# Two transformer blocks: the first four modulation weight blocks as TensorE products with silu(c) as one column

## The chip, the cores and the metric

One core of a Trainium2 chip runs the whole program; the other cores are idle. The metric is the device time of one execution in microseconds (us). Three runs of the kernel before took 1876.26, 1877.37 and 1877.62 us; the median is 1877.37 us.

## What is computed

Two blocks follow each other on a sequence of 256 positions with 1024 features. The first block is modulated by a vector `c` of 1024 numbers. What matters here is its start, layer 0:

```python
def first_block(x, c, ...):
    c_act = jax.nn.silu(c)
    h = layer_norm(x)
    for l in range(DEPTH):                              # DEPTH = 2
        ada = (c_act @ w_ada[l] + b_ada[l])[:, None, :]
        sh1, sc1, g1, sh2, sc2, g2 = jnp.split(ada, 6, axis=-1)
        u = h * (1.0 + sc1) + sh1
        y = mixer(u, w_in[l], ...)                      # z = u @ w_in, and so on
        ...
```

All arrays are float32. `w_ada[l]` is 1024 x 6144, `w_in[l]` is 1024 x 10768: the weights are by far the most data (385 MB are read in all), and the products with them most of the work.

## The kernel before, in words

**Weights.** Every weight matrix is cut on the host into chunks of 128 x 2048 numbers (1 MB), in the one order in which the kernel uses them: the list `plan` (`make_plan`, L133). SyncE loads chunk after chunk into a tile `raw` with three buffers (`emit_load`, L434; the DMA is L444 for the first three chunks, in two halves each, and L446 for all others). So a chunk can start to load when the chunk three places ahead of it has been used up. For a chunk of an ordinary matrix, ScalarE writes a rounded copy `hi` (L475, fp32r) and VectorE the remainder `lo = raw - hi` (L475); each product is then three TensorE passes: `hi` with the rounded activation `uh`, `lo` with `uh`, `hi` with the remainder `ul` (`mv_part`, L555 to L557).

**Modulation.** A chunk `("ada", l, sec, q)` holds the columns of `w_ada` for 256 of the 1024 outputs of one of the six sections, with outputs on the partitions. `ada_step` (L406) has VectorE multiply it by `crow`, silu(c) spread over all partitions, and sum over the free axis, 1024 products for 128 outputs in one instruction (L414, two to a chunk).

**The start.** `plan` begins: ada sc1 and sh1 of quarter q=0 (chunks 0 and 1), two chunks of the mixer's first products m_o and m_v (2 and 3), ada of q=1 (4 and 5), a mixer chunk (6), ada of q=2 (7, 8), two mixer chunks, ada of q=3, and so on. `norm_u0` (L836) normalizes `x` on VectorE (`bn_stats` L789, then L860), spreads `c` over the partitions with two TensorE products of a row of halves (`cbc`, L855), takes its tanh on ScalarE (L856) and builds `crow` (L862); TensorE transposes the normalized x into four PSUM banks (`tr`, L864). `step(g)` then makes the columns 2g and 2g+1 of `u`: `us` = 1 + sc (L871), one half of `uf` on VectorE (L873), the other on ScalarE (L874), the rounded `uh` on ScalarE (L877), the remainder `ul` on VectorE (L878). Each step needs one quarter of the modulation. With step 0 done, the first 24 products `mvh` can start (chunks 2 and 3, first halves); with step 1 the next ones.

**Unread products.** `busy` (L882) issues products of a tile of ones whose result nobody reads: 12 ahead of the first `mvh`, 24 behind these 24.

**Order.** The part that `norm_u0` issues is pinned: each of TensorE, VectorE and ScalarE keeps the order in which the code issues it. Behind it a scheduler of the framework places instructions by priority, and may slip some in, such as the first four products `smz` (L939) of the small gate projection. Each engine works through its own queue strictly in order.

Of the kernel before, what the change touches and what calls it, by code (L numbers as in the profile page):

```python
# [12 lines left out]
AF = mybir.ActivationFunctionType  # L13
ALU = mybir.AluOpType
AX = mybir.AxisListType

P = 128
T = 256
D = 1024
# [110 lines left out]
    return out + list(main[last:])  # L130


def make_plan():  # L133
    first = [("ada", 0, SEC[n], q) for q in range(4) for n in ("sc1", "sh1")]
    plan = []
    for l in range(DEPTH):
        m1 = spread(mixer1_chunks(l), ada_chunks(l, ["g1", "sc2", "sh2"]), *ADA1)
        plan += m1 if l else (first[:2] + m1[:2] + first[2:4] + m1[2:3] + first[4:6] + m1[3:5] +
                                 first[6:] + m1[5:])
        nxt = ada_chunks(l + 1, ["sc1", "sh1"]) if l + 1 < DEPTH else []  # L140
        plan += spread(ffn1_chunks(l), ada_chunks(l, ["g2"]) + nxt, *ADA2)
    for l in range(DEPTH):
        plan += mixer2_chunks(l) + ffn2_chunks(l)
    return plan
# [18 lines left out]
def host_arrays(inp):  # L163
# [20 lines left out]
    for i, d in enumerate(plan):  # L184
        kind, l = d[0], d[1]
        a = d[2:]
        if kind == "ada":
            c = a[0] * D + a[1] * 256 + r(256)
            o = w["w_ada"][l][:, c].T.reshape(2, P, D).transpose(1, 0, 2).reshape(P, -1)
        elif kind == "m_o":  # L190
            o = pack(w["w_in"][l], a[1] * 4 + r(4), 3072 + a[0] * 512 + r(512))
        elif kind == "m_v":
            o = pack(w["w_in"][l], a[1] * 4 + r(4), 2048 + a[0] * 512 + r(512))
        elif kind == "m_q":
            o = pack2(w["w_in"][l], k8, a[0] * 256 + r(256))
        elif kind == "m_k":
            o = pack2(w["w_in"][l], k8, 1024 + a[0] * 256 + r(256))
        elif kind == "a_v":
            o = pack(w["w_in"][l], a[1] * 4 + r(4), 4112 + 3072 + a[0] * 512 + r(512))
        elif kind == "a_qk":  # L200
            q0 = 4112 + a[1] * 512 + a[0] * 128 + r(128)
            o = pack2(w["w_in"][l], k8, np.concatenate([q0, q0 + 1536]))
        elif kind == "gab":
            o = pack(w["w_in"][l], a[1] * 4 + r(4), 4112 + 4608 + (a[0] % 2) * 1024 + (a[0] // 2) * 512 + r(512))
        elif kind == "w_b":
            o = pack(w["w_b"][l], r(4), a[0] * 512 + r(512))
        elif kind == "w_a":
            o = pack(w["w_a"][l], a[1] * 4 + r(4), a[0] * 512 + r(512))
        elif kind == "w_o":
            o = pack(w["w_out"][l], a[1] * 4 + r(4), a[0] * 512 + r(512))  # L210
        elif kind == "w13":
            c = a[0] * 128 + r(128)
            o = np.concatenate([pack(w["w1"][l], k8, c), pack(w["w3"][l], k8, c)], axis=1)
        elif kind == "w13p":
            f = np.concatenate([w[nm][l][:, P * j:P * j + P] for j in range(2) for nm in ("w1", "w3")], axis=1)
            o = pack(f, a[0] * 4 + r(4), r(512))
        elif kind == "upp":
            c = np.concatenate([o_ + P * j + r(P) for j in range(2) for o_ in (0, DFF)])
            o = pack(w["w_up_2"][l], a[0] * 4 + r(4), c)
        elif kind == "zp":  # L220
            o = pack(w["w_in_2"][l], a[0] * 4 + r(4), r(512))
        elif kind == "w2":
            o = units(w["w2"][l], w2_units(a[0]))
        elif kind == "x":
            o = pack2(w["w_in_2"][l], k8, 1024 + a[0] * 256 + r(256))
        elif kind == "k2":
            o = pack2(w["w_in_2"][l], k8, 2592 + 1024 + r(256))
        elif kind == "v2":
            o = pack(w["w_in_2"][l], k8, 2592 + 1280 + r(256))
        elif kind == "q2":  # L230
            c = np.concatenate([2592 + 64 * h + r(64) for h in order[4 * a[0]:4 * a[0] + 4]])
            o = pack2(w["w_in_2"][l], k8, c)
        elif kind == "z":
            o = pack2(w["w_in_2"][l], k8, a[0] * 256 + r(256))
        elif kind == "w_o2":
            o = units(w["w_out_2"][l][rows_o2], wo2_units(a[0]))
        elif kind == "up":
            c = a[0] * 128 + r(128)
            o = pack2(w["w_up_2"][l], k8, np.concatenate([c, DFF + c]))
        elif kind == "down":  # L240
            o = units(w["w_down_2"][l], w2_units(a[0]))
        else:
            raise ValueError(kind)
        ws[i] = o
# [59 lines left out]
def two_blocks_kernel(ctx: ExitStack, tc: tile.TileContext, a: dict, out: bass.AP, stop=None):  # L304
# [28 lines left out]
    def lbank(name):  # L333
        return lin.tile([P, 512], F32, tag="lin", name=name)
# [4 lines left out]
        nc.sync.dma_start(x[:, tt], a["x"][:, tt])  # L339
    crow = tmp([D], "crow")  # L340
    trow = tmp([D], "trow")
    c1 = tmp([D], "crow1", parts=1)
    S.dma_start(c1, a["crow"])
    S.dma_start(cst[:, :P], a["cst"][:, :P])
# [62 lines left out]
    def ada_step(d, raw):  # L407
        _, l, sec, q = d
        if q == 0:
            ada[l, sec] = tmp([8], f"adap{sec}", bufs=1)  # L410
        for i in range(2):
            ct = 2 * q + i
            src = raw[:, i * D:(i + 1) * D]
            V.tensor_tensor_reduce(src, src, crow, 1.0, pv1[l][:, 136 + sec * 8 + ct:137 + sec * 8 + ct], ALU.mult,  # L414
                                   ALU.add, ada[l, sec][:, ct:ct + 1])
        if sec not in (2, 5) or q < 3:
            return
        gt = tmp([D], "grow", bufs=2)
        col = ada[l, sec]
        ada[l, sec] = gt  # L420

        def spread_rows():
            for hf in range(2):
                ps = bank("adag")
                for c in range(4):
                    PE.transpose(ps[:, c * P:(c + 1) * P], col[:, 4 * hf + c:4 * hf + c + 1].to_broadcast([P, P]), ident)
                S.activation(gt[:, hf * 512:(hf + 1) * 512], ps, AF.Copy)

        ada_wait.append([4, spread_rows])

    ada_wait = []

    def emit_load(i, hold=None):
        d = plan[i]  # L434
# [401 lines left out]
    def norm_u0():  # L836
# [1 line left out]
        u = new_u()  # L838
        stats = tmp([2, 2, 6], "lnst")
        trs = [bank("tr") for _ in range(4)]  # L840
        sil = []
        mvs = []
        for tt in range(2):
            for hf in range(2):
# [4 lines left out]
            V.tensor_scalar(rs, mv[:, 1:2], LN_EPS, None, ALU.add)  # L849
            powm(rs, rs, 1)  # L850
            mvs.append((mv, rs))
        for hf in range(2):
            h = slice(hf * 512, (hf + 1) * 512)
            ps = lbank("cbc")
            PE.matmul(ps, halves_, c1[:, h], start=True, stop=True)  # L855
            S.activation(trow[:, h], ps, AF.Tanh)  # L856
            sil.append((h, ps))
        for tt in range(2):
            mv, rs = mvs[tt]
            V.tensor_scalar(x[:, tt, :], x[:, tt, :], mv[:, 0:1], rs, ALU.subtract, ALU.mult)  # L860
            h, ps = sil[tt]
            V.scalar_tensor_tensor(crow[:, h], trow[:, h], 1.0, ps, ALU.add, ALU.mult)  # L862
            for ct in range(8):
                PE.transpose(trs[ct // 2][:, (ct % 2) * T + tt * P:(ct % 2) * T + (tt + 1) * P],  # L864
                             x[:, tt, ct * P:(ct + 1) * P], ident)
# [11 lines left out]
            S.activation(u[0][:, c, :], uf, AF.Copy)  # L877
            V.tensor_tensor(u[1][:, c, :], uf, u[0][:, c, :].bitcast(F32), ALU.subtract)  # L878

        outs = [[lbank("mvh") for _ in range(2)] for _ in range(2)]  # L880

        def busy(o, n):  # L882

            for _ in range(n):
                PE.matmul(o[:, :P], ones, ones, start=True, stop=True)

        busy(outs[0][0], 12)
        st["cap"] = 4
        ensure(2)
        hold = []  # L890
        emit_load(2, hold)
        st["emitted"] = 3
# [1 line left out]
        step(0, hold[1])  # L894
        hold[2]()
        hold[3]()
        ws = [chunk(*d, 0) for d in EARLY[:2]]
        for w, o in zip(ws, outs):
            for tt in range(2):
                mv_part(0, w[0], tt, u, o, False, 0, 3)  # L900
        busy(trs[0], 24)
        st["cap"] = len(plan)
        return u, (step, ws, outs)

    def log1p_exp_neg(xin, n, tag):

# [65 lines left out]
    def mixer1(l, u, ob0=None, small=None, begun=None):  # L972
# [172 lines left out]
        for hp in range(2):  # L1145
# [4 lines left out]
            if l == 0:  # L1150
                if hp == 0:
                    vs = [tmp([2, 512], "mv") for _ in range(2)]
                    step, ws, obs = begun
                    dst = [oth[:, :, :512], vs[0], oth[:, :, 512:], vs[1], vt[:, 0]]
                    ensure(6)
                    step(1)
                    for i, d in enumerate(EARLY):
                        if i in (2, 4):
# [278 lines left out]
    for l in range(DEPTH):  # L1437
        pv = pv1[l]
        if l == 0:
            with pinned():  # L1440
                u, begun = norm_u0()
            stats, tail = mixer1(l, u, begun=begun)
        else:
            small = small_weights(a["wg"][l])
            u, outs = cross(tail, ln_norm(stats, u_coef(l, 0, gb)), [("m_o", l, 0, kh) for kh in range(2)],
                            TR1[0])
            for n, fn in zip((3, 6, 9, 12), affine(l - 1, 1)):
                defer(n, fn)
            stats, tail = mixer1(l, u, outs, small)
# [535 lines left out]
```

## Time and profile before

| what | value |
|---|---|
| median of three runs | 1877.37 us |
| the profiled execution, its own time | 1877.16 us |
| its span, first to last instruction | 1875.4 us |
| TensorE busy | 1847.4 us (99%) |
| VectorE busy | 1470.6 us (78%) |
| ScalarE busy | 1083.4 us (58%) |
| mean granted TensorE clock | 0.999 |
| HBM read | 384.82 MB |

The span is 1.8 us shorter than the execution's time; what lies around it is launch and end. PE is TensorE's products, PEld its weight loads, which overlap products. A TensorE instruction is recorded from its start to the end of its pipeline, so what it costs in a stream is the distance between starts, not its recorded length.

### The profile page before, as it was taken

The numbers are of one execution on the slowest core, as the hardware profiler recorded it, in microseconds if no ns is written. First come the engines' busy times: TensorE is split into PE (matmuls) and PEld (weight loads), VectorE is DVE, ScalarE is ACT, GpSimd is POOL, SyncE is SP. The second block draws the span as 40 slices with busy tenths as digits, with TensorE's granted clock in tenths as the row PEclk, the third lists the DMA queues.
The fourth block names the chain that finished last, engine by engine and source line by source line (L and its number), as shares of the span: only waits on it lengthen the run. The fifth ranks groups of instructions, "written<-read, shape, count | busy, mean of one in ns | idle before, by whom it ended". The sixth has DMA issues, their size and how long they took to land.

```text
span 1875.4 us, 31504 instructions
## 1 busy us (share of the span) xinstructions
PE 1847.4 (99%) x12422; PEld 1668.0 (89%) x12422; DVE 1470.6 (78%) x2581; ACT 1083.4 (58%) x1889; POOL 58.1 (3%) x96
## 2 busy tenths in 40 slices
PE   8999999999999999999999999999999999999998
PEld 6889988899988899988899879877999899889996
DVE  8888877788757878877876579997876599978763
ACT  4566654454445566554544456895654569956552
POOL 0000000000000000000000000000000000000000
PEclk9999999999999999999999999999999999999999
DMA  8744677467855445766477635544645465445452
GB/s 323 261 180 157 249 265 282 181 258 284 286 196 202 177 163 192 280 252 262 159 257 270 238 145 190 174 125 157 225 181 188 152 213 178 133 186 202 181 187 82
DMA packets 64341, 388.01 MB, mean 207 GB/s; under 512 B 7627, under 2 KB 12539, under 8 KB 21698
## 3 DMA queue, kind: packets, MB, share of 16 engines
q1 hardware_dynamic: 58064, 364.93, 53.2%
q0 software_dynamic: 4832, 20.13, 3.6%
q8 instruction: 97, 1.59, 0.3%
q10 hardware_dynamic: 1298, 0.95, 0.2%
q14 instruction: 50, 0.41, 0.1%
HBM read 384.82 MB, written 5.36 MB: 208 GB/s over the span
## 4 chain that ended last, share of the span: by engine, by line
PE 84%; DVE 6%; ACT 5%; issue 3%; DMA 1%; POOL 0%; POOLq 0%; DVEq 0%; ACTq 0%
PE lst L522 14%; PE lst L524 14%; PE lst L523 14%; PE ffo L616 4%; PE ffo L614 4%; PE ffo L615 4%; PE wo L615 1%; PE wo L614 1%; PE wo L616 1%; DVE lo L475 1%; PE gabl L555 1%; PE gabl L556 1%; PE gabl L557 1%; PE sy L1628 1%; PE avl L556 1%
## 5 line engine op out<-in xcount | busy, mean ns | idle before, releaser
L475 ACT ACTIVATE hi<-raw 128x1024 fp32r<-128x1024 f32 x546 | 571.7, 1057 | 486.8 <-PE lst L523 254.4
L475 DVE TENSOR_TENSOR lo<-raw,hi 128x1024 fp32r<-128x1024 f32 x546 | 662.6, 1222 | 226.2 <-ACT hi L475 222.3
L522 PE MATMUL lst<-uh,hi 128*128 128x256 f32 x2336 | 668.7, 286 | 0.4 <-DVE q2t L1786 0.4
L524 PE MATMUL lst<-uh,lo 128*128 128x256 f32 x2336 | 664.4, 284 | 0.1
L523 PE MATMUL lst<-ul,hi 128*128 128x256 f32 x2336 | 663.7, 284 | 0.0
L522 PEld LDWEIGHTS lst<-uh,hi 128*128 128x128 f32 x2336 | 447.8, 192 | 3.6 <-issue 2.1
L524 PEld LDWEIGHTS lst<-uh,lo 128*128 128x128 f32 x2336 | 447.8, 192 | 2.0 <-issue 1.2
L523 PEld LDWEIGHTS lst<-ul,hi 128*128 128x128 f32 x2336 | 448.0, 192 | 1.1 <-issue 0.3
L614 PE MATMUL ffo<-hi,ffh 128*128 128x512 f32 x352 | 137.3, 390 | 0.0
L615 PE MATMUL ffo<-lo,ffh 128*128 128x512 f32 x352 | 137.0, 389 | 0.0
L616 PE MATMUL ffo<-hi,ffl 128*128 128x512 f32 x352 | 137.0, 389 | 0.0
L414 DVE CUSTOM_DVE_ANT_0 raw<-raw,crow,pv 128x1024 f32<-128x1024 f32 x96 | 121.1, 1281 | 14.3 <-DMA raw<-in_ws_dram 14.0
L965 DVE SCALAR_TENSOR_TENSOR cacc<-cin,pv,cacc 128x254 f32<-128x254 f32 (+2 forms) x272 | 112.5, 477 | 0.2 <-ACT cacc L958 0.2
L616 PEld LDWEIGHTS ffo<-hi,ffl 128*128 128x128 f32 x352 | 66.1, 188 | 13.8
L615 PEld LDWEIGHTS ffo<-lo,ffh 128*128 128x128 f32 x352 | 66.1, 188 | 13.5
L614 PEld LDWEIGHTS ffo<-hi,ffh 128*128 128x128 f32 x352 | 66.1, 188 | 13.5
L555 PE MATMUL gabl<-hi,uh 128*128 128x512 f32 x128 | 51.2, 400 | 0.0
L557 PE MATMUL gabl<-hi,ul 128*128 128x512 f32 x128 | 50.4, 394 | 0.0
L556 PE MATMUL gabl<-lo,uh 128*128 128x512 f32 x128 | 50.3, 393 | 0.0
L1610 ACT ACTIVATE sM<-arow,ac 128x128 f32<-128x128 f32 x128 | 45.3, 392 | 0.0
L1457 ACT ACTIVATE rsq<-xres 128x512 f32<-128x512 f32 x20 | 12.5, 627 | 47.7 <-DVE xres L1932 21.6
L773 ACT ACTIVATE uf<-tr,ub,us 128x128 f32<-128x128 f32 x36 | 14.4, 452 | 36.9 <-PE tr L759 36.9
(396 smaller groups left out, 3005.9 us busy)
## 6 DMA issues: line engine op xcount, KB each, us to landing
raw<-in_ws_dram SPq DMA_DIRECT2D x329, 1024.0 KB, 4.9
abias<-in_bt_dram SPq DMA_DIRECT2D x32, 256.0 KB, 5.0
arow<-scra POOLq DMA_DIRECT2D x32, 256.0 KB, 4.6
wtab<-skew SPq DMA_DIRECT2D x16, 384.0 KB, 3.2
gb<-in_rows_dram POOLq DMA_DIRECT2D x8, 512.0 KB, 6.3
skew<-scrt POOLq DMA_DIRECT2D x4, 1024.0 KB, 11.6
raw<-in_ws_dram SPq DMA_DIRECT2D x6, 512.0 KB, 9.2
grow<-scrg POOLq DMA_DIRECT2D x2, 1024.0 KB, 6.5
```

What stands on the lines that cost most here:

```text
L414: V.tensor_tensor_reduce(src, src, crow, 1.0, pv1[l][:, 136 + sec * 8 + ct:137 + sec * 8 + ct], ALU.mult, ALU.add, ada[l, sec][:, ct:ct + 1])
L475: fn()
L522: PE.matmul(outp, sh, mh, start=first, stop=False)
L523: PE.matmul(outp, sh, ml, start=False, stop=False)
L524: PE.matmul(outp, sl, mh, start=False, stop=last)
L555: PE.matmul(outs[tt], sl[0], hi[:, i, :], start=kt == first, stop=False)
L556: PE.matmul(outs[tt], sl[0], lo[:, i, :], start=False, stop=False)
L557: PE.matmul(outs[tt], sl[1], hi[:, i, :], start=False, stop=kt == last)
L614: PE.matmul(o, sh, hi[:, i, :], start=kt in first, stop=False)
L615: PE.matmul(o, sh, lo[:, i, :], start=False, stop=False)
L616: PE.matmul(o, sl, hi[:, i, :], start=False, stop=kt in last)
L965: V.scalar_tensor_tensor(acc[:, c, lo:hi], src[:, lo + s:hi + s], cw[:, k0 + j:k0 + j + 1], acc[:, c, lo:hi], ALU.mult, ALU.add)
```

## The change

The four chunks of q = 0 and q = 1 (table `ADA_PE`) are packed as ordinary weights, with the 1024 inputs on the partitions. TensorE multiplies them with silu(c) laid out as a tile `ccol` of 128 x 8: eight products of one column for each 128 outputs, 16 to a chunk, into spare corners of PSUM banks; VectorE adds the bias of two columns in one instruction (L424 of the changed kernel). `ccol` comes from eight small products of `c` itself (`cc`), a tanh and one VectorE instruction. `crow` is still built, later, for the quarters 2 and 3 and the other sections, which stay on VectorE. The unread products are 6 ahead of the first `mvh` and 8 behind the new products of q = 1. The gate projection's weights are prepared behind the first mixer chunks, and not early as before.

```diff
+ADA_PE = [("ada", 0, SEC[n], q) for q in range(2) for n in ("sc1", "sh1")]
...
-        if kind == "ada":
+        if kind == "ada" and d in ADA_PE:
+            o = pack(w["w_ada"][l], k8, a[0] * D + a[1] * 256 + r(256))
+        elif kind == "ada":
...
+    ccol = tmp([8], "ccol")
...
+        if d in ADA_PE:
+            c = slice(2 * q, 2 * q + 2)
+            ps = ada_ps[q][:, 2 * (sec == SEC["sc1"]):][:, :2]
+            for j in range(2):
+                for k in range(8):
+                    PE.matmul(ps[:, j:j + 1], raw[:, k * 256 + j * P:k * 256 + (j + 1) * P], ccol[:, k:k + 1],
+                              start=k == 0, stop=k == 7)
+            V.tensor_tensor(ada[l, sec][:, c], ps, pv1[l][:, 136 + sec * 8 + 2 * q:138 + sec * 8 + 2 * q], ALU.add)
+            return
...
+        outs = [[lbank("mvh") for _ in range(2)] for _ in range(2)]
+        cc = outs[0][0][:, :8]
+        cbc = outs[0][1], outs[1][0]
+        ada_ps[0], ada_ps[1] = outs[1][1][:, :4], trs[0][:, :4]
+        for k in range(8):
+            PE.matmul(cc[:, k:k + 1], c1[:, k * P:(k + 1) * P], halves_[:, 0:1], start=True, stop=True)
+        for hf in range(2):
+            PE.matmul(cbc[hf], halves_, c1[:, hf * 512:(hf + 1) * 512], start=True, stop=True)
+        S.activation(ccol, cc, AF.Tanh)
+        V.scalar_tensor_tensor(ccol, ccol, 1.0, cc, ALU.add, ALU.mult)
+        for hf in range(2):
+            h = slice(hf * 512, (hf + 1) * 512)
+            S.activation(trow[:, h], cbc[hf], AF.Tanh)
+            S.activation(crow[:, h], cbc[hf], AF.Copy)
+        st["cap"] = 4
         mvs = []
...
-        for hf in range(2):
-            h = slice(hf * 512, (hf + 1) * 512)
-            ps = lbank("cbc")
-            PE.matmul(ps, halves_, c1[:, h], start=True, stop=True)
-            S.activation(trow[:, h], ps, AF.Tanh)
-            sil.append((h, ps))
         for tt in range(2):
             mv, rs = mvs[tt]
             V.tensor_scalar(x[:, tt, :], x[:, tt, :], mv[:, 0:1], rs, ALU.subtract, ALU.mult)
-            h, ps = sil[tt]
-            V.scalar_tensor_tensor(crow[:, h], trow[:, h], 1.0, ps, ALU.add, ALU.mult)
+        for tt in range(2):
+            ensure(tt + 1)
             for ct in range(8):
...
-                PE.matmul(o[:, :P], ones, ones, start=True, stop=True)
-
-        busy(outs[0][0], 12)
-        st["cap"] = 4
-        ensure(2)
+                PE.matmul(o, ones, ones, start=True, stop=True)
+
+        busy(outs[0][0][:, :P], 6)
...
         hold[3]()
+        for hf in range(2):
+            h = slice(hf * 512, (hf + 1) * 512)
+            V.scalar_tensor_tensor(crow[:, h], trow[:, h], 1.0, crow[:, h], ALU.add, ALU.mult)
+        small = small_weights(a["wg"][0])
         ws = [chunk(*d, 0) for d in EARLY[:2]]
...
-        busy(trs[0], 24)
         st["cap"] = len(plan)
-        return u, (step, ws, outs)
+        return u, (step, ws, outs, partial(busy, trs[0][:, T:T + P], 8)), small
...
                     ensure(6)
+                    busy()
                     step(1)
```

How this moves instructions shows at three places. Line numbers of the changed kernel are its own. The first is TensorE from its first product to the first `mvh`; `crow_84` and `crow_85` are the row of `c`, `raw` a weight chunk. Before:

```order
L855 MATMUL cbc<-crow_84,halves 128x512 x2
L864 MATMUL tr<-cst,xres 128x128 x16
L885 MATMUL mvh<-ones 128x128 x12
L555 MATMUL mvh<-hi,uh 128x512
L556 MATMUL mvh<-lo,uh 128x512
```

and now:

```order
L862 MATMUL mvh<-halves,crow_85 128x1 x8
L864 MATMUL mvh<-crow_85,halves 128x512 x2
L422 MATMUL mvh<-ccol,raw 128x1 x16
L888 MATMUL tr<-cst,xres 128x128 x8
L422 MATMUL mvh<-ccol,raw 128x1 x16
L888 MATMUL tr<-cst,xres 128x128 x8
L907 MATMUL mvh<-ones 128x128 x6
L571 MATMUL mvh<-hi,uh 128x512
```

Eight small products stand ahead of `cbc`, and the 32 products of chunks 0 and 1 around the first eight transposes.

The second is TensorE between the first 24 `mvh` and the next ones. Before:

```order
L557 MATMUL mvh<-hi,ul 128x512
L885 MATMUL tr<-ones 128x128 x24
L939 MATMUL smz<-uh,sw 64x256
L939 MATMUL smz<-ul,sw 32x256 x2
L939 MATMUL smz<-uh,sw 64x256
L555 MATMUL mvh<-hi,uh 128x512
```

and now:

```order
L573 MATMUL mvh<-hi,ul 128x512
L422 MATMUL tr<-ccol,raw 128x1 x32
L907 MATMUL tr<-ones 128x128 x8
L571 MATMUL mvh<-hi,uh 128x512
L572 MATMUL mvh<-lo,uh 128x512
```

The 32 products of chunks 4 and 5 come first, then eight unread ones; the four `smz` stand some 50 products further on.

The third is VectorE from step 0 to the remainders of chunk 3 (`adap` is the modulation, `sw` the gate weights). Before:

```order
L871 TENSOR_SCALAR us_191<-adap_174 128x2
L977 TENSOR_SCALAR gnh<-pv_0_99 128x8
L873 TENSOR_SCALAR uf<-tr,us_191,adap_180 128x256
L876 TENSOR_TENSOR lo<-raw,hi 128x1024
L878 TENSOR_TENSOR ul<-uf,uh 128x512
L896 TENSOR_TENSOR lo<-raw,hi 128x1024
L475 TENSOR_TENSOR lo<-raw,hi 128x1024 x2
```

and now:

```order
L424 TENSOR_TENSOR adap_155<-mvh,pv_0_100 128x2
L424 TENSOR_TENSOR adap_184<-mvh,pv_0_100 128x2
L895 TENSOR_SCALAR us_224<-adap_155 128x2
L1000 TENSOR_SCALAR gnh<-pv_0_100 128x8
L897 TENSOR_SCALAR uf<-tr,us_224,adap_184 128x256
L900 TENSOR_TENSOR lo<-raw,hi 128x1024
L902 TENSOR_TENSOR ul<-uf,uh 128x512
L916 TENSOR_TENSOR lo<-raw,hi 128x1024
L919 SCALAR_TENSOR_TENSOR crow<-trow,crow 128x512 x2
L952 TENSOR_TENSOR sw<-swr,sw 128x8x32
L491 TENSOR_TENSOR lo<-raw,hi 128x1024 x2
```

Two instructions for `crow` and one for `sw` now stand between the remainder of chunk 2 and the two of chunk 3. SyncE's and GpSimd's queues keep their order, and all engines keep theirs behind their first few hundred instructions.

## Rows read from the trace of the kernel before

**Rows 1.** The page: busy time of each engine over the span.

```profile
PE 1847.4 (99%) x12422; PEld 1668.0 (89%) x12422; DVE 1470.6 (78%) x2581; ACT 1083.4 (58%) x1889; POOL 58.1 (3%) x96
```

**Rows 2.** Windows: stretch, length, busy and count of PE, PEld, DVE, ACT, POOL; clock.

```profile
10.00:13.70 3.70, 3.70 (x18) 3.70 (x19) 3.67 (x6) 0.00 (x0) 0.34 (x1) 1.00 1.02 416
...
30.90:80.00 49.10, 49.10 (x255) 41.89 (x256) 41.62 (x64) 30.15 (x41) 0.59 (x1) 1.00 0.83 310
```

**Rows 3.** The chain of waits up to 31 us: start, length, what.

```profile
15.59 1.20 DVE raw L414
...
16.98 0.55 DVE uf L873
...
17.56 0.57 ACT uf L874
...
18.16 0.63 ACT uh L877
...
28.28 0.47 DVE uf L873
```

**Rows 4.** Timeline of PE: start, length, operation; in brackets idle before, releaser.

```profile
3.27 3.75 PE L855 MATMUL cbc<-crow,halves 1*128 1x512 f32 x4 [3.27 <-DMA crow<-in_crow_dram]
9.99 3.68 PE L864 MATMUL tr<-cst,xres 128*128 128x128 f32 x16 [2.96 <-DVE xres L860]
13.46 3.22 PE L885 MATMUL mvh<-ones 128*128 128x128 f32 x24
18.84 0.50 PE L555 MATMUL mvh<-hi,uh 128*128 128x512 f32 x1 [2.17 <-ACT uh L877]
...
24.82 5.52 PE L885 MATMUL tr<-ones 128*128 128x128 f32 x48
30.10 0.36 PE L939 MATMUL smz<-uh,sw 128*64 128x256 f32 x1
...
30.86 0.50 PE L555 MATMUL mvh<-hi,uh 128*128 128x512 f32 x1
```

**Rows 5.** Timeline of PEld, the weight loads of the transposes.

```profile
9.98 3.28 PEld L864 LDWEIGHTS tr<-cst,xres 128*128 128x128 f32 x16 [4.54 <-DVE xres L860]
```

**Rows 6.** Timeline of PE in the second block: four products of one column.

```profile
1262.99 0.95 PE L1661 MATMUL gss<-ones,gsq 128*128 128x1 f32 x8
1263.86 0.87 PE L1628 MATMUL sy<-sM,xd 128*64 128x256 f32 x6
```

**Rows 7.** Loads of chunk 0's halves, then chunk 1's: issue, us to landing.

```profile
L444 SPq DMA_DIRECT2D raw<-in_ws_dram x2: 424/484/543, 1.6 to 2.1; - x2
...
DMA to landing us min/median/max: 7.8/8.2/8.6
...
L444 SPq DMA_DIRECT2D raw<-in_ws_dram x2: 456/552/649, 2.7 to 3.4; - x2
...
DMA to landing us min/median/max: 9.2/9.2/9.2
```

**Rows 8.** Timeline of DVE.

```profile
4.46 1.29 DVE L789 BATCH_NORM_STATS2 lnst<-xres 128x6 f32<-128x512 f32 x2 [3.18 <-DMA xres<-in_x_dram]
...
7.10 0.43 DVE L929 TENSOR_TENSOR sw<-swr,sw 128x256 fp32r<-128x256 f32 x1 [0.45 <-ACT sw L928]
...
9.13 0.80 DVE L860 TENSOR_SCALAR xres<-xres,lnmv,lnrs 128x1024 f32<-128x1024 f32 x1
...
11.17 0.68 DVE L862 SCALAR_TENSOR_TENSOR crow<-trow,cbc 128x512 f32<-128x512 f32 x1
...
19.77 1.23 DVE L896 TENSOR_TENSOR lo<-raw,hi 128x1024 fp32r<-128x1024 f32 x1 [0.26 <-ACT hi L895]
20.91 2.35 DVE L475 TENSOR_TENSOR lo<-raw,hi 128x1024 fp32r<-128x1024 f32 x2
```

**Rows 9.** Timeline of ACT, the rounding of chunk 2's first half.

```profile
14.54 1.06 ACT L893 ACTIVATE hi<-raw 128x1024 fp32r<-128x1024 f32 x1 [6.50 <-DMA raw<-in_ws_dram]
```

**Rows 10.** An addition from PSUM on DVE: count, duration in ns, starts.

```profile
L990 DVE TENSOR_TENSOR zgs<-smt,bg x2: 176/176/176, 73.0 to 578.5; 128x32 f32<-128x32 f32 x2
```

More of the change, by code (lines that the diff above doesn't have):

```diff
@@ L431, in two_blocks_kernel @@
     ada_wait = []
+    ada_ps = {}
     def emit_load(i, hold=None):
@@ L840, in norm_u0 @@
         trs = [bank("tr") for _ in range(4)]
-        sil = []
+        outs = [[lbank("mvh") for _ in range(2)] for _ in range(2)]
[13 more added lines that the diff above has]
+        st["cap"] = 4
         mvs = []
@@ L878, in step @@
             V.tensor_tensor(u[1][:, c, :], uf, u[0][:, c, :].bitcast(F32), ALU.subtract)
-        outs = [[lbank("mvh") for _ in range(2)] for _ in range(2)]
         def busy(o, n):
             for _ in range(n):
-                PE.matmul(o[:, :P], ones, ones, start=True, stop=True)
-        busy(outs[0][0], 12)
-        st["cap"] = 4
-        ensure(2)
+                PE.matmul(o, ones, ones, start=True, stop=True)
+        busy(outs[0][0][:, :P], 6)
         hold = []
@@ L1152, in mixer1 @@
                     vs = [tmp([2, 512], "mv") for _ in range(2)]
-                    step, ws, obs = begun
+                    step, ws, obs, busy = begun
                     dst = [oth[:, :, :512], vs[0], oth[:, :, 512:], vs[1], vt[:, 0]]
                     ensure(6)
+                    busy()
                     step(1)
@@ L1440, in two_blocks_kernel @@
             with pinned():
-                u, begun = norm_u0()
-            stats, tail = mixer1(l, u, begun=begun)
+                u, begun, small = norm_u0()
+            stats, tail = mixer1(l, u, small=small, begun=begun)
         else:
```

## The prediction

> **What bounds the kernel now.** I read the page's busy times first: TensorE is busy for 1847.4 us of the span [rows 1], so about 28 us in all are there to win by waiting less; anything else must take work off TensorE. The windows come next: from 30.9 us to 80 us TensorE is busy for 49.10 of 49.10 us while VectorE has 41.62 [rows 2]. So from the second group of `mvh` on TensorE is the bound, and the change touches only what lies ahead: what counts is **when TensorE starts the first `mvh` (18.84 us) and the second group (30.86 us)**, and what useful work it has done by then [rows 4]. A delay there is carried to the end; a start earlier is a gain.
>
> Before 31 us the chain of waits shows who decides: VectorE's sums of the modulation, 1.20 us each, the last of the first four from 15.59 us to 16.79 us, then `uf` on VectorE, `uf` on ScalarE, `uh`, one after the other [rows 3]. From the start of VectorE's `uf` (16.98) to the first product (18.84) are 1.86 us [rows 3, 4]. TensorE meanwhile waits 3.27 us for `c`, 2.96 us for the normalized x, and 2.17 us for `uh` [rows 4]; the 48 instructions of unread products from 24.82 us fill a wait too. The change takes the eight sums, some 9.7 us, off VectorE, and puts products on TensorE. Do these cost TensorE less than the waits that they replace?
>
> **Price of a product of one column.** The trace has one row of this very form: four float32 products with 128 x 128 weights and one column are recorded as eight instructions, and the next product starts 0.87 us later, 0.109 us per instruction [rows 6]. It is a price at the full clock. The unread products of 128 columns cost 5.28 us for 48, 0.110 us each [rows 4], so the missing columns save nothing: the weights set the pace. Early in the program instructions take longer: the weight loads of the 16 transposes from 9.98 us take 3.28 us, 0.205 us each [rows 5], although the window's granted clock reads 1.00 [rows 2]. The 24 unread instructions from 13.46 us begin at such a pace and then halve it, and `cbc`, 0.94 us for 512 columns [rows 4], is at the slow one too. So I read the rows up to about 14 us as 1.2 GHz and those behind as 2.4 GHz, and the bounds of one instruction are 0.109 us and 0.205 us.
>
> **First part: up to the first `mvh`.** TensorE gets `c` at 3.27 us [rows 4].
> - `cc`: 8 products, 16 instructions, 1.7 to 3.3 us. It stands where `cbc` was slow, so 3.3 us: until 6.6 us. No row has one-partition weights with one column.
> - `cbc`: 3.75 us as before, or half at the higher clock: until 8.5 to 10.3 us.
> - Chunk 0 lands in halves at 1.6 + 7.8 = 9.4 us and 2.1 + 8.6 = 10.7 us [rows 7]. Of its 32 instructions eight can run on the first half; the other 24 follow at 0.109 us, until 13.3 us, or until 13.8 us if `cbc` ends only at 10.3 us. I take 13.5 us.
> - Eight transposes, 0.9 us at 0.110 us: 14.4 us. Their x is later than before, as the statistics stand behind `ccol` on VectorE: the first `bn_stats` ran at 4.46 us and x was ready from 9.13 + 0.80 us [rows 8]; now they begin at about 7.3 us (6.6 plus the end of a product, a tanh and one small VectorE instruction), and x is ready near 11.2 us, hidden behind chunk 0.
> - Chunk 1 landed by 3.4 + 9.2 = 12.6 us [rows 7], so nothing waits; 32 instructions, 3.5 us: 17.9 us.
> - Then about 0.2 us for the last product to end, 0.18 us for the bias [rows 10], 0.19 us as before between the modulation and `uf` (16.79 to 16.98), and the 1.86 us: first `mvh` at 20.3 us. The second eight transposes and the six unread products lie beside that.
>
> The eight sums, 11.88 to 16.79 us in part, are gone, yet the first group starts **1.5 us later**: VectorE did them beside TensorE's transposes, and TensorE now has them all in its own row.
>
> **Second part: the 24 products.** Their second dozen needs the remainder `lo` of chunk 3. VectorE started it 1.14 us behind that of chunk 2 (19.77, 20.91) [rows 8], just in time. Now two instructions for `crow`, 0.6 us each when in a row, and `sw`, 0.4 us [rows 8], stand between them. Both starts move with the first `mvh`, so TensorE waits about **1.6 us** longer in the middle of the group. (They were early and hidden before; here they are queued ahead of what TensorE waits for.)
>
> **Third part: up to the second group.** From the end of the 24 products to the second group it took 30.86 - 24.82 = 6.04 us, filled with unread products and four `smz`. Now it is 64 instructions, 64 x 0.109 = 7.0 us, and then 0.2 + 0.18 + 1.86 = 2.2 us for bias, `uf`, `uf`, `uh`, under which the eight unread products (16 instructions, 1.8 us) lie: 9.2 us, **3.2 us more**. Taking 22 of 36 unread products away gives nothing by itself: they filled waits. Chunk 5 loads later (its buffer waits for chunk 2's remainder), but TensorE reaches it only 3.5 us into this block. The four `smz`, from 30.10 to about 30.56 us in a wait so far, move into the dense stretch: **0.45 us more**.
>
> The sum is 1.5 + 1.6 + 3.2 + 0.45 = **6.8 us slower**, 5.0 to 7.5 us with the bounds above (the low end takes `cbc` at the higher clock and 0.101 us per instruction, the distance between the eight starts of [rows 6] if the last is counted to its own end). Against the profiled execution's 1877.16 us that is 1884.0 us; this execution lies 0.2 us under the median, so the forecast for the median is also **1884.0 us**, within 1882 to 1886. Steps 2 and 3 of `u` stay on VectorE and keep their distance to TensorE, which is as late as they are. Differences under 0.2%, 3.75 us, can't be told from none here.
>
> **Rival 1: the lower clock holds for longer (slower still).** For it: all early rows are slow, even after 3.75 us of unbroken `cbc` [rows 4], and the fast pace came only behind four unbroken microseconds of transposes and unread products of 128 columns. A column per weight load may keep TensorE as good as idle for whatever sets the clock. Against it: TensorE would now be at work from 3.27 us with hardly a gap. If the pace halves at 14.2 us as before, chunk 0's products run from 10.3 to 15.6 us (19 slow, 13 fast), the first `mvh` starts at 22.4 us, and the sum is 8.9 us: 1886 us. If the whole start is slow, chunks 0 and 1 take 6.6 us each, the transposes 1.6 us, the first `mvh` is at 27.5 us, and with 64 slow instructions in the third part (6.1 us more) the sum is some 20 us: 1897 us. The Trainium skill, "TensorE: Matmul & The Clock Gate", section "A second HAM failure mode: psum-queue depth-cycling", says that small idle times between groups of matmuls can make the clock fall back; no row before shows that for products of one column.
>
> **Rival 2: the products cost far less (not slower).** The sum holds 56 instructions ahead of the first `mvh` on the path and 64 behind it; each 0.01 us less takes 1.2 us off. It breaks even at 0.109 - 6.8/120 = 0.053 us, half the row's price, as if each product loaded its weights once and not twice. There is a floor below: chunk 2 lands at 14.54 us, ScalarE rounds it until 15.6 us ahead of its `uf` and `uh` [rows 9], 1.2 us, so the first `mvh` can't start before 16.9 us (1.9 us earlier than now). With free products the sum would be -1.9 + 1.6 + (2.2 - 6.04) + 0.45 = -3.7 us: 1873.7 us, just what counts as no change. So this rival gives 1873.7 to 1877 us. Against it: the gss row has the same form. The same page of the Trainium skill, section "Back-to-back issue gap", lists some 25 ns for products of up to 64 columns taken alone; by that, as an estimate, the sum would be -2.1 us, 1875.3 us. The row of this trace says four times that, since each instruction brings its own weights.
>
> **Rival 3: VectorE's 9.7 us show up later (faster).** A later wait for VectorE would shrink. Against it: none up to 80 us [rows 2], and VectorE's order is the same behind the start.
>
> **How the numbers follow.** The forecast has 0.52; rival 1 has 0.26, spread between 1886 and 1897 us; rival 2 0.14, nearly all within 0.2%; rival 3 and what I don't see 0.08, split evenly. That makes slower 0.80, within 0.2% 0.14, faster 0.06. The range reaches down to 1877 us to take in the dearer end of rival 2 and up to 1894 us for most of rival 1.
>
> **What would show it.** In the profile after: products of one column (`ccol`, `raw`) at 0.109 us apart in the third part, 7.0 us for 64; the first `mvh` at about 20.3 us and the second group at about 37 us; a wait of TensorE for `lo` in the middle of the first 24; TensorE without a gap from there to 80 us. Starts 0.2 us apart behind 14 us would be rival 1; 0.05 us apart, rival 2. I am wrong if the second group starts before 31 us.

## The result: 1.2% slower, and the profile after

The changed kernel takes 1900.82 us, median of four runs (1899.03 to 1901.28), against 1877.49 us before: a ratio of 1.0122, 95% interval 1.0109 to 1.0134. That is **23.3 us slower**, in the direction that was forecast, but three times the forecast 6.8 us and outside the range (1877 to 1894). The profiled execution took 1900.45 us, its span 1898.7 us: 23.3 us over the span before as well.

The timeline of TensorE after shows where it goes (columns as in [rows 4]; every one-column product is two instructions):

```profile
2.23 3.54 PE L862 MATMUL mvh<-halves,crow 1*128 1x1 f32 x16 [2.23 <-DMA crow<-in_crow_dram]
5.63 3.76 PE L864 MATMUL mvh<-crow,halves 1*128 1x512 f32 x4
9.39 6.96 PE L422 MATMUL mvh<-ccol,raw 128*128 128x1 f32 x32
16.22 1.95 PE L888 MATMUL tr<-cst,xres 128*128 128x128 f32 x8
17.96 6.83 PE L422 MATMUL mvh<-ccol,raw 128*128 128x1 f32 x32
24.64 1.95 PE L888 MATMUL tr<-cst,xres 128*128 128x128 f32 x8
26.38 2.00 PE L907 MATMUL mvh<-ones 128*128 128x128 f32 x12
28.14 0.48 PE L571 MATMUL mvh<-hi,uh 128*128 128x512 f32 x1
...
32.09 0.50 PE L572 MATMUL mvh<-lo,uh 128*128 128x512 f32 x1 [0.73 <-DVE lo L491]
...
34.72 4.14 PE L422 MATMUL tr<-ccol,raw 128*128 128x1 f32 x32
39.11 6.99 PE L422 MATMUL tr<-ccol,raw 128*128 128x1 f32 x32 [0.25 <-DVE adap L424]
46.35 3.78 PE L907 MATMUL tr<-ones 128*128 128x128 f32 x16 [0.25 <-DVE adap L424]
49.79 0.77 PE L571 MATMUL mvh<-hi,uh 128*128 128x512 f32 x1
```

The first `mvh` starts at 28.14 us, 9.3 us later than in [rows 4]; the second group at 49.79 us, 18.9 us later. The blocks of chunks 0 and 1 take 6.8 us each, 0.21 us an instruction: the slow pace of [rows 5], from the first product to past 26 us. In the third part TensorE starts the first 28 instructions by 37.65 us, their starts 0.11 us apart; the four that are left of that block and the next 32 start 0.21 us apart. The windows (columns as in [rows 2]) name the cause there:

```profile
18.00:24.60 6.60, 6.60 (x33) 6.60 (x33) 0.00 (x0) 0.00 (x0) 0.00 (x0) 1.00 0.34 142
...
34.70:37.60 2.90, 2.90 (x28) 2.88 (x26) 0.00 (x0) 0.00 (x0) 0.00 (x0) 1.00 0.79 328
37.60:38.80 1.20, 1.20 (x7) 1.17 (x6) 0.00 (x0) 0.00 (x0) 0.00 (x0) 0.52 0.00 0
39.10:46.10 7.00, 6.99 (x32) 6.90 (x32) 0.16 (x1) 0.00 (x0) 0.00 (x0) 0.50 0.39 150
46.30:51.30 5.00, 4.95 (x20) 4.66 (x21) 3.35 (x4) 3.09 (x4) 0.00 (x0) 0.50 0.61 211
51.40:60.00 8.60, 8.60 (x40) 7.07 (x39) 5.63 (x11) 2.40 (x4) 0.00 (x0) 1.00 0.82 322
```

From about 37.6 us to 51.3 us the granted clock is 0.50, the 1.2 GHz level. It fell within the run of one-column products and came back behind the unread ones. TensorE was busy without a gap where it fell (1.20 of 1.20 us from 37.60 us on); its last wait before, 0.73 us for `lo`, had ended at 32.09 us. The first window needs care: it reads 1.00, with 33 instructions in 6.6 us, as many per microsecond as the windows at 0.50 have. The record of the granted clock begins only with its first change, here near 27.4 us, and up to there the column says 1.00; the spacing alone tells.

Two rows of ScalarE show what else lies in these waits (when `uh` was ready):

```profile
26.52 0.63 ACT L901 ACTIVATE uh<-uf 128x512 fp32r<-128x512 f32 x1
...
47.58 0.63 ACT L901 ACTIVATE uh<-uf 128x512 fp32r<-128x512 f32 x1
```

`uh` was there at 27.15 us and 48.2 us, 1.0 and 1.6 us before the products that wait for it could start: the unread products, meant to fill the wait, ran at the slow pace themselves and stood in the way.

### The profile page after: what moved, and what is told of

The parts are those of the page before. It is cut to its first block, busy times and chain, and to the rows that moved or that the text cites. A ratio compares the mean times of both kernels' runs of the same rounds, so it can differ in the third digit from the quotient of the medians.

```text
span 1898.7 us, 31700 instructions
## 1 busy us (share of the span) xinstructions
PE 1873.5 (99%) x12522; PEld 1693.1 (89%) x12522; DVE 1461.7 (77%) x2570; ACT 1084.7 (57%) x1892; POOL 57.9 (3%) x96
## 4 chain that ended last, share of the span: by engine, by line
PE 86%; ACT 5%; DVE 5%; issue 3%; DMA 1%; POOL 0%; POOLq 0%; ACTq 0%; DVEq 0%; SPq 0%
PE lst L538 14%; PE lst L540 14%; PE lst L539 14%; PE ffo L632 4%; PE ffo L630 4%; PE ffo L631 4%; PE gabl L571 2%; PE gabl L572 2%; PE gabl L573 2%; PE wo L631 1%; PE wo L630 1%; PE wo L632 1%; DVE lo L491 1%; PE sy L1652 1%; ACT hi L491 1%
## 5 line engine op out<-in xcount | busy, mean ns | idle before, releaser
L429 DVE CUSTOM_DVE_ANT_0 raw<-raw,crow,pv 128x1024 f32<-128x1024 f32 x88 | 111.4, 1281 | 24.3 <-DMA raw<-in_ws_dram 24.2
```

## The experiments

The theory after the result: the clock stays low, and falls again, while TensorE works on products of one column; the sum's other terms are about right. Rivals: fresh weights or the transfers make the products slow; the clock depends on weight loads alone; or the first part is lost for another reason.

**128 equal columns in place of one.** Of the 64 modulation products only the moving operand changes, and with it the width of what they write:

```diff
-                    PE.matmul(ps[:, j:j + 1], raw[...], ccol[:, k:k + 1], ...)
+                    PE.matmul(pb[:, j * n:(j + 1) * n], raw[...],
+                              ccol[:, k:k + 1].to_broadcast([P, n]), ...)      # n = 128
```

> The changed kernel with one edit: the vector of silu(c) is read 128 times (a broadcast of the one column), so each of the 64 products of the modulation streams 128 equal columns and not one; only the first is read. Weight loads, number of instructions, waits and loads stay. Theory (TensorE's clock does not rise, and falls, while it streams single columns): the spacing of the first blocks halves before 15 us, the first mvh starts near 22 us and not 28.1 us, the clock stays up in the third part, the second group starts near 37 us and not 49.8 us, and the time is 1883 to 1887 us. Rival (the early products are slow because their weights have just been loaded, or the clock depends on weight loads alone): spacing 0.2 us as before the edit, time 1897 us or more.

Measured: 1886.84 us (1.0046 of before, 1.0031 to 1.0061). More arithmetic, the same number of instructions, **14.0 us less** than the changed kernel. TensorE's timeline:

```profile
10.16 5.66 PE L424 MATMUL mvh<-ccol,raw 128*128 128x128 f32 x32
15.65 1.03 PE L891 MATMUL tr<-cst,xres 128*128 128x128 f32 x8
16.52 3.74 PE L424 MATMUL mvh<-ccol,raw 128*128 128x128 f32 x32
...
22.50 0.50 PE L574 MATMUL mvh<-hi,uh 128*128 128x512 f32 x1
...
25.84 1.94 PE L424 MATMUL tr<-ccol,raw 128*128 128x128 f32 x16
...
32.37 3.84 PE L424 MATMUL tr<-ccol,raw 128*128 128x128 f32 x32 [0.25 <-DVE adap L427]
...
40.31 0.50 PE L574 MATMUL mvh<-hi,uh 128*128 128x512 f32 x1 [0.70 <-ACT uh L904]
```

The pace doubles within the first block, the second block takes 3.6 us and not 6.7 us, and 32 instructions of the third part take 3.8 us. The second group comes later than expected (40.31 against 37 us). Some 1.6 us of that are VectorE's: the scheduler put a sum of the next quarter, which first waits for its load, ahead of `uf`:

```profile
37.18 1.28 DVE L432 CUSTOM_DVE_ANT_0 raw<-raw,crow,pv 128x1024 f32<-128x1024 f32 x1 [0.43 <-DMA raw<-in_ws_dram]
...
38.39 0.54 DVE L900 TENSOR_SCALAR uf<-tr,us,adap 128x256 f32<-128x256 f32 x1
```

So the rivals on weights and transfers fall: the weight loads and the transfers are the same in both kernels. One thing besides the pace did not stay, against what I had expected: from 25.84 us the scheduler has 16 instructions of chunk 4 within the 24 `mvh`, where the changed kernel waited for `lo`, and the four `smz` stand ahead of the second group again. The rows show the pace; that all of the 14.0 us is pace they do not show.

**The same for chunks 4 and 5 alone** (`n = 128` where q is 1, else 1).

> The changed kernel with 128 equal columns for the products of chunks 4 and 5 only; chunks 0 and 1 keep one column. Theory: the first mvh stays at 28.1 us; the third part runs at the full clock, so its 64 instructions take 7 us and not 11.4 us, the second group starts near 43.5 us and at full pace, and the time is 1892 to 1894 us. Rival (the fall in the third part has another cause than the single columns): unchanged, 1900 us.

Measured: 1893.82 us (1.0085, 1.0070 to 1.0100), 7.0 us under the changed kernel. TensorE:

```profile
18.86 6.83 PE L424 MATMUL mvh<-ccol,raw 128*128 128x1 f32 x32
...
35.65 3.73 PE L424 MATMUL tr<-ccol,raw 128*128 128x128 f32 x32
39.63 3.84 PE L424 MATMUL tr<-ccol,raw 128*128 128x128 f32 x32 [0.25 <-DVE adap L427]
...
45.63 0.50 PE L574 MATMUL mvh<-hi,uh 128*128 128x512 f32 x1
```

The start is slow as in the changed kernel; the third part is not. Here the order up to the second group is the changed kernel's. So the cost falls about half to each: 7.0 us in the third part, 7.0 us more when the first blocks get columns too (the first run's changes of order are within the latter).

**Chunks 0 and 1 alone on TensorE** (`range(1)` in `ADA_PE`; 24 unread products behind the 24 `mvh`, as before).

> The changed kernel with only chunks 0 and 1 on TensorE; chunks 4 and 5 are summed on VectorE as in the kernel before, and 24 unread products stand behind the first 24 mvh as there. It shows what the first half of the change costs alone. Theory: first mvh at 28.1 us, at full clock from there on, second group near 41.5 us against 30.9 us before: 1887 to 1889 us. Rival (the first part's delay is hidden again, since VectorE is free earlier): under 1884 us.

Measured: 1889.55 us (1.0061, 1.0046 to 1.0076), 12.1 us slower than before; a little over what was expected, since `c` came at 3.21 us in the profiled run (2.23 us in the changed kernel's) and the first `mvh` at 29.7 us. The second group's delay is the first's, nothing is hidden:

```profile
29.74 0.67 PE L571 MATMUL mvh<-hi,uh 128*128 128x512 f32 x1
...
41.70 0.50 PE L571 MATMUL mvh<-hi,uh 128*128 128x512 f32 x1
```

**The kernel before with one-column unread products.** Here not even a reader is involved:

```diff
-                PE.matmul(o[:, :P], ones, ones, start=True, stop=True)
+                PE.matmul(o[:, :1], ones, ones[:, 0:1], start=True, stop=True)
```

> The kernel before with one edit: its 36 unread products stream one column of ones and not 128. Nothing reads them, nothing waits for them, and each loads the same weights. Theory: the clock rises later than 14.2 us, the first mvh run at half speed for some microseconds, and the clock may fall again in the second run of unread products: 3 to 8 us slower, 1880 to 1886 us. Rival (single columns with their weight loads keep the clock as 128 columns do): no change, 1877.5 us.

Measured: 1881.92 us in ten runs (1.0022, 1.0012 to 1.0031), 4.5 us slower. Timeline of TensorE and, below it, windows:

```profile
13.11 5.12 PE L885 MATMUL mvh<-ones 128*128 128x1 f32 x24
18.50 0.80 PE L555 MATMUL mvh<-hi,uh 128*128 128x512 f32 x1 [0.27 <-ACT uh L877]
...
26.82 6.23 PE L885 MATMUL tr<-ones 128*128 128x1 f32 x48
...
34.01 0.63 PE L555 MATMUL mvh<-hi,uh 128*128 128x512 f32 x1
```

```profile
24.40:31.20 6.80, 6.80 (x53) 6.35 (x51) 5.19 (x10) 2.77 (x4) 0.00 (x0) 1.00 1.02 422
31.20:38.00 6.80, 6.74 (x24) 5.70 (x24) 6.69 (x12) 0.81 (x2) 0.00 (x0) 0.50 0.73 275
```

The 24 instructions that took 3.22 us [rows 4] take 5.12 us; the first `mvh`, on time at 18.50 us, run at half speed for six microseconds; and the clock falls to 0.50 again in the second run of unread products. The clock's part is shown without any of the change's other edits.

**Without the six unread products ahead of the first `mvh`** (the call is taken out of the changed kernel).

> The changed kernel without its six unread products ahead of the first mvh (those behind the products of chunks 4 and 5 stay). In its profile they run at half speed from 26.4 us and end only at 28.1 us, while uh was there at 27.2 us. Theory (single columns leave the clock low, and only products that stream columns raise it): the first mvh starts near 27.2 us but at half speed, as the clock rises only behind it; the 24 mvh take 1.5 to 3.5 us longer, and the wait for lo among them, 0.7 us, is lost in that: 1900 to 1904 us. Rival (the six only stand in the way): first mvh at 27.2 us at full speed, 1899.5 to 1900.5 us.

Measured: 1901.12 us (1.0125, 1.0111 to 1.0139), no different from the changed kernel:

```profile
27.71 0.80 PE L571 MATMUL mvh<-hi,uh 128*128 128x512 f32 x1 [0.62 <-ACT uh L901]
...
35.22 4.38 PE L422 MATMUL tr<-ccol,raw 128*128 128x1 f32 x32
```

The first `mvh` no longer waits for unread products, but runs at half speed, and the 24 end at 35.2 us (34.7 us with the six; half a microsecond here is a wait of chunk 0's products for their load). So these six take about what they give. Whether more of them would have helped was not tried.

**Chunks 4 and 5 alone, with 128 columns**, on the kernel before; `ccol` is made behind `cbc`, with GpSimd in VectorE's place.

> The kernel before with chunks 4 and 5 alone on TensorE, each product reading silu(c) 128 times so that 128 columns stream; crow is built early as before, the column of silu(c) is made behind cbc (two small operations on ScalarE, two on GpSimd); 12 unread products ahead of the first mvh as before and eight behind the new products. It prices the third part alone at the full clock. Theory (the sum's term is right when the clock holds): first mvh at 18.8 to 19.4 us, 64 instructions in 7.0 us, second group 3 to 4 us later than before: 1880.5 to 1882 us. Rival (VectorE's relief hides part of it): under 1879.5 us.

Measured: 1885.02 us (1.0041, 1.0027 to 1.0055): **a miss**, 7.5 us where 3 to 4.5 us were expected. I had added the bias for each 128 outputs by itself, and TensorE's next products, in the same PSUM bank, waited each time:

```profile
24.70 1.95 PE L424 MATMUL tr<-ccol,raw 128*128 128x128 f32 x16
26.89 2.05 PE L424 MATMUL tr<-ccol,raw 128*128 128x128 f32 x16 [0.25 <-DVE adap L426]
29.20 2.05 PE L424 MATMUL tr<-ccol,raw 128*128 128x128 f32 x16 [0.25 <-DVE adap L426]
32.09 2.05 PE L424 MATMUL tr<-ccol,raw 128*128 128x128 f32 x16 [0.84 <-DVE adap L426]
...
36.20 0.47 PE L571 MATMUL mvh<-hi,uh 128*128 128x512 f32 x1
```

The second group is 5.3 us late, of which four waits are 1.6 us (the fourth ahead of the unread products). The work itself keeps its price, 0.11 us an instruction, at a clock that never fell. Another 1.7 us of the profile's 7.2 us arise in the second block. Near 1559 us VectorE waits 2.75 us for a transfer, `wtab`, where it waited 0.80 us in the kernel before; TensorE then waits 1.2 us for `qP` and 0.4 us more for `sM`. Why that transfer came later stays open.

**Only what fits into TensorE's waits.** The kernel before, with the second 128 outputs of chunks 1 and 5 on TensorE (eight products each, 128 columns) in the place of unread products; ten unread ones behind chunk 5's, in the second run four.

```diff
+            if i and d in ADA_PE:                     # ADA_PE: sh1, q = 0 and 1
+                for k in range(8):
+                    PE.matmul(ada_ps[q], src[:, k * P:(k + 1) * P], ccol[:, k:k + 1].to_broadcast([P, P]),
+                              start=k == 0, stop=k == 7)
+                V.tensor_tensor(ada[l, sec][:, ct:ct + 1], ada_ps[q][:, 0:1], pv1[l][...], ALU.add)
+                continue
```

> The kernel before with two eighths of the modulation of q=0 and q=1 on TensorE: of chunks 1 and 5 the second 128 outputs, as eight products each that stream 128 equal columns, in the place of unread products; everything else stays on VectorE, and 20 unread products are left. VectorE does three sums in place of four in each quarter. Theory (what TensorE can do inside its waits is a gain, what exceeds them a loss): first mvh near 18.0 us, second group near 29 us, 0.5 to 2 us faster: 1875.5 to 1877 us. Rival (the eight single-column products of c, now in the wait ahead of the transposes, keep the clock down for longer): 1878.5 us or more.

> The kernel of the run before with four instead of ten unread products behind the new products of chunk 5. There they ended at 30.3 us, while uh was ready at 29.3 us. Three of the small smz products slip back into this stretch. Theory (unread products behind the last wait stand in the way): second group near 29.6 us, 1.0 to 1.4 us faster than with ten: 1877.5 to 1878.5 us, no different from the kernel before. Rival (the second group waits for something else, chunk 6 or ul): no change, 1879.3 us.

Measured: 1879.28 us with ten, 1879.18 us with four, both 1.0010 of before (1.0001 to 1.0019), eleven runs each between 1876.6 and 1882.3 us. TensorE, with ten and then with four:

```profile
13.57 2.88 PE L423 MATMUL mvh<-ccol,raw 128*128 128x128 f32 x16
...
18.67 0.50 PE L570 MATMUL mvh<-hi,uh 128*128 128x512 f32 x1 [0.89 <-ACT uh L900]
...
30.33 0.48 PE L570 MATMUL mvh<-hi,uh 128*128 128x512 f32 x1
```

```profile
18.62 0.50 PE L570 MATMUL mvh<-hi,uh 128*128 128x512 f32 x1 [0.89 <-ACT uh L900]
...
29.21 0.41 PE L570 MATMUL mvh<-hi,uh 128*128 128x512 f32 x1
```

The first `mvh` gains 0.2 us, not the 0.8 us that I expected: the pace doubled only within these 16 instructions, so they took 2.7 us. The second group gains 0.5 us and 1.65 us. Even the latter is given back: in that profile TensorE's first `avl` starts at 96.5 us, against 96.1 us before, so 2.1 us are lost on the way. There are waits where [rows 2] have none:

```profile
52.70 0.73 PE L570 MATMUL mvh<-hi,uh 128*128 128x512 f32 x2 [0.21 <-ACT hi L490]
53.97 0.50 PE L571 MATMUL mvh<-lo,uh 128*128 128x512 f32 x1 [0.53 <-DVE lo L490]
...
72.55 0.61 PE L969 MATMUL smt<-ident,smzs 64*128 64x16 f32 x4 [0.55 <-DVE smzs L966]
```

TensorE, started earlier, waits for the rounded parts of the weights and for `smzs`: 1.3 us of the 2.1 us. Products under TensorE's old waits cost little, then (1.8 us, 0.1%), but nothing tried beats the kernel before.

The profiled execution with ten took 1882.33 us, 3.0 us over its median, and shows one thing more:

```profile
120.14 2.67 PE L1135 MATMUL mo<-mv,mPT 128*128 128x256 f32 x8 [2.16 <-ACT mPT L1128]
```

Behind this wait the granted clock is 0.50 from 121.3 to 124.7 us. The profile of the second run (1896.15 us, 2.3 us over its median) has the same from 91.7 to 95.1 us, behind a wait of 2.06 us for `smzs`. So this case has falls behind idle time too, with no one-column products near, and these two profiles are dearer than their kernels' medians.

## Why the prediction was wrong

**What bounds the kernel** held in the main: TensorE's two starts decide most of it. Before, the first `avl` started at 96.1 us, after at 118.7 us; 22.6 of the 23.3 us are there by then, 18.9 us of them at the start of the second group. Behind it the forecast had 0.45 us for `smz` and TensorE "without a gap". In the rows it waits four times where the kernel before does not, for `lo`, `hi`, `lo` and `smzs`, 1.4 us in all and 2.4 us with the slower starts around the waits; the longest is

```profile
76.52 0.50 PE L572 MATMUL mvh<-lo,uh 128*128 128x512 f32 x1 [0.52 <-DVE lo L491]
```

In the first run, with 128 columns, none of these four waits is there.

**The price of one instruction** held where the clock was up: 0.11 us in the first 28 of the third part, and 0.11 us with 128 columns.

**The step that failed is the first part's clock.** I took 2.4 GHz from about 10 us on, because TensorE "would now be at work from 3.27 us with hardly a gap", and carried that level through the third part. In the rows, being busy did not raise the clock between 2.23 us and 26 us, with one-partition products, one-column products and eight transposes between the two blocks, and in the third part it fell while one-column products ran. The reason against rival 1 was wrong, not its arithmetic: its milder case (pace halving at 14.2 us, first `mvh` at 22.4 us, 8.9 us in all) is what the run with 128 columns did: 22.50 us, 9.4 us. That the totals lie so close is partly luck: 1.6 us of the 9.4 us are VectorE's sum, which no term had. Its full case (27.5 us, some 20 us) is the changed kernel: 28.14 us, 23.3 us. I gave the rival 0.26 and then ended the range under its full case.

**The terms**, predicted at the full clock and measured:
- First `mvh`: 1.5 us later; measured 9.3 us, of which 1.0 us is unread products at half speed. Counted from the arrival of `c`, 1.0 us earlier in this profile than in [rows 4], it is 10.3 us.
- The wait for `lo`: 1.6 us; measured 0.73 us, and the 24 products take 6.58 us where they took 5.98 us. VectorE and ScalarE used the time that TensorE spent on the unread products. The place was right, the size not.
- Third part: 9.2 us in place of 6.04 us; measured 15.07 us. With 128 columns (second run) it is 45.63 - 35.65 = 10.0 us; my sum lacked two waits of 0.25 us of TensorE for the bias additions, which use the bank that the next products write.
- I had not seen that the second group itself would start at half speed: about 0.7 us more until 51.3 us.
- The bounds of the sum, worked out again from the same terms, are some 5.5 to 7.1 us and not 5.0 to 7.5 us; the miss does not hang on that.

**Rival 2** (cheap products) fell: one column costs what 128 do. The Trainium skill, "TensorE: Matmul & The Clock Gate", section "Back-to-back issue gap", has some 25 ns for products of few columns taken alone; the rows here have 0.11 us and more an instruction, each with its weight load. **Rival 3** fell too: VectorE's busy time over the span sank from [rows 1]'s 1470.6 to 1461.7 us, but nothing is won back later: TensorE is 22.6 us late at its first `avl` and 23.3 us at the end.

On rival 1 the same page of the Trainium skill (section "A second HAM failure mode: psum-queue depth-cycling") spoke of idle moments between groups that let the clock oscillate; this trace shows a fall without idle time, with TensorE busy for 1.20 of 1.20 us around it (37.60 to 38.80 us).

## What to carry to other kernels

Price a moved piece of work at the clock that it leaves behind: behind one-column products it was low here, and reading the same column 128 times gave 14 us back, about as much as the products' own time at the full clock (128 instructions of 0.11 us). Look for the pace in the distances between starts, as busy time and an early granted clock of 1.00 both hide it. And unread products are only free while the wait that they fill lasts longer than they do at the pace that they get.

## What the runs showed of the hardware

- A float32 product with 128 x 128 weights costs the same for one column as for 128: two instructions, 0.11 us each at 2.4 GHz, 0.21 us at 1.2 GHz.
- TensorE's granted clock fell from 1.00 to 0.50 (1.2 GHz) while the engine was busy without a gap: near 37.6 us in the changed kernel, with nothing but one-column products running, and at 31.2 us in the kernel before with unread products of one column. With 128 columns in the same places (first and second run) it did not fall there. It also fell behind waits of 2.06 us and 2.16 us in two profiles (the second run, and the run with ten unread products).
- Products with one partition of weights (`cc`, `cbc`) ran at the slow pace throughout in every profile shown here (7.2 us of them in the changed kernel, from 2.23 to 9.39 us). They also come first in every one, so the runs do not tell which of the two it is.
- A product into a PSUM bank that VectorE is about to read in another place waited 0.25 us or more for it each time (0.84 us once); this is how the program orders them, and I did not try it without.
